# The beginning of a two-layer trunk: loads, squares and the order of the first norm

## Chip, cores, metric

One core of one Trainium2 chip. The metric is the device time of one execution in microseconds (us); the median of several runs is compared.

## What is computed

The reference runs two layers of a decoder trunk on x (1024 tokens by 1024 channels, float32). Each layer normalises x (`_rms`: x divided by the root of its mean square, times a gain per channel), projects it by one wide matrix, feeds three mixers (differential attention, a recurrent mixer, cross-attention to a memory of 256 tokens), gates and adds them, projects again and adds the result to x. Ahead of the cross-attention the memory is normalised and projected once for each layer:

```
h = _rms(x, norm_g[l]);  proj = h @ w_in[l]
mem_kv = _rms(mem, mem_norm_g[l]) @ w_mem_kv[l]
```

Only the beginning is touched by the change: the norm of x for the first layer and the memory's K and V for both layers.

## The kernel before, in words

The kernel is written with a scheduler that takes the operations in the order of the program, gives each a rank in that order, and lays out a fixed list for each engine from its own estimate of durations, the lowest rank first among what is ready. On the chip each engine works through its list in order and waits where an input is missing. `tc.high_priority()` sets the rank of what is inside back to that of the start of the program. Tensors are kept with the channels on the 128 partitions, x as 8 channel blocks (`NK`) of 1024 tokens, in two halves of 512 tokens.

Products are made in a split form: a float32 matrix becomes a rounded part `hi` (made by ACT, L178) and the rest `lo` (a subtraction, L171, on POOL or DVE), and `product` (L214) adds three matmuls for each channel block: hi by hi, hi by lo, lo by hi. `weight` (L204) loads 512 KB on the SP queue into `w_raw` and splits it into `w_hi` and `w_lo`; each of the three has two buffers, shared by all weights of the kernel, so the load of a third weight waits for the `w_lo` of the first, and the split of a third weight for the product of the first.

The prologue, ahead of both layers, does this in program order. (1) Eight loads of x on ACT's queue, each two channel blocks of half the tokens (512 KB). (2) `memory_load`: the small parameters `par`, the memory `mt` (1 MB) and the constants `con`, on SP's queue. (3) `gqk`, a product of two parameter columns on DVE, and `memory` for layer 0: `mh` on ACT and `ml` on DVE, eight times 128x256, the memory times its gain in split form. (4) The norm of x, a half at a time: ACT squares each channel block (L1143), PE sums the squares over the channels with matmuls by a column of ones (`token_sums`, four matmuls for each block, adding up over eight blocks in `ps_x`; the profile counts two records for each), DVE makes the reciprocal root of the mean (`rsqrt`, twelve small operations from `rs_v` to `h_r`), ACT and PE spread it over the partitions (`spread`, four transposes into `ps_rb`, a copy `rbs`), and `normed` makes for each block `h_t` on DVE, `hh` on ACT and `hl` on DVE, or on POOL for every third block. (5) `memory_norm`, the same for the memory, with squares added up on DVE (`acc`). (6) `memory` for layer 1. (7) `memory_kv` for each layer: eight weights, eight products of 24 matmuls with 256 columns, a copy out of PSUM (ACT, L401) and a multiplication by the norm (`kv`, DVE); `memory_store` normalises K, transposes V and stores both.

The weights and the PSUM copies of `memory_kv` already stand under `tc.high_priority()`. After the prologue comes layer 0, which begins with `project` of the first input weights: matmuls `ps_pj<-hh,w_hi` with 512 columns.

Of the kernel before, what the change touches and what calls it, by code (L numbers as in the profile page):

```python
# [11 lines left out]
F32 = mybir.dt.float32  # L12
# [3 lines left out]
AF = mybir.ActivationFunctionType  # L16
ALU = mybir.AluOpType
AX = mybir.AxisListType

P = 128  # L20
S = 1024
D = 1024
DEPTH = 2
NK = D // P
# [16 lines left out]
              caq=1, cak=1, daq=1, dak=1, sub=1)  # L41
PC, _o = {}, 0
# [88 lines left out]
def trunk(ctx, tc, io, out, layers=DEPTH, dump=None):  # L131
    nc = tc.nc
    PSUM, DRAM = bass.MemoryType.PSUM, bass.MemoryType.DRAM

    cp = ctx.enter_context(tc.tile_pool(name="cp", bufs=1))
# [6 lines left out]
    pa = ctx.enter_context(tc.tile_pool(name="pa", bufs=2, space=PSUM))  # L142
# [5 lines left out]
    par = cp.tile([P, DEPTH, NPAR], F32, name="par")  # L148
# [5 lines left out]
    ones = cp.tile([P, 1], F32, name="ones")  # L154
# [15 lines left out]
    def ttv(o, a, b, op, eng=None):  # L170
        (eng or nc.vector).tensor_tensor(o, a, b, op=op)  # L171

    def stt(o, a, s, b, op0, op1):
        nc.vector.scalar_tensor_tensor(o, a, s, b, op0=op0, op1=op1)  # L174

    def split(hi, lo, src, eng=None):

        nc.scalar.activation(hi, src, AF.Copy)  # L178
        ttv(lo, src, hi.bitcast(F32), ALU.subtract, eng)
# [20 lines left out]
    def weight(src, eng=None, wp=wp):  # L200
        raw = wp.tile([P, 8 * P], F32, name="w_raw", tag="w_raw", bufs=2)
        hi = wp.tile([P, 8 * P], F32R, name="w_hi", tag="w_hi", bufs=2)
        lo = wp.tile([P, 8 * P], F32R, name="w_lo", tag="w_lo", bufs=2)
        nc.sync.dma_start(raw, src.rearrange("p k c -> p (k c)"))  # L204
        split(hi, lo, raw, eng or nc.gpsimd)
        return (hi.rearrange("p (k c) -> p k c", k=src.shape[1]),
                lo.rearrange("p (k c) -> p k c", k=src.shape[1]))

    def product(ps, w, act, nk, cols, toks):

        n = 0
        for k in range(nk):
            for a, b in ((0, 0), (0, 1), (1, 0)):
                nc.tensor.matmul(ps, w[a][:, k, cols], act[b][:, k, toks],  # L214
                                 start=n == 0, stop=n == 3 * nk - 1)
                n += 1

    def half(h):
        return slice(h * 512, h * 512 + 512)
# [28 lines left out]
    def transpose(o, i):  # L248
        nc.tensor.transpose(o, i, ident)  # L249

    def token_sums(ps, sq, n, rhs, first=True, last=True):

        c = rhs.shape[-1]
        for j in range(n):
            nc.tensor.matmul(ps[:, j * c:(j + 1) * c], sq[:, j * P:(j + 1) * P], rhs,
                             start=first and j == 0, stop=last, skip_group_check=True)
# [16 lines left out]
    def spread(ps, col, n, c):  # L273

        b = tp.tile([P, 512], F32, name="spread", tag="ta", bufs=TA)
        bv = b[:, :n * P].rearrange("p (j c f) -> p j c f", j=n, c=c)
        nc.scalar.copy(bv, col.rearrange("p (j c) -> p j c", c=c).unsqueeze(3).to_broadcast([P, n, c, P // c]))
        for j in range(n):
            transpose(ps[:, j * P:(j + 1) * P], b[:, j * P:(j + 1) * P])

    def pcol(l, name, i=0):
        return par[:, l, PC[name][0] + i:PC[name][0] + i + 1]
# [13 lines left out]
    def normed(l, hf, x1, r, rp, hh, hl):  # L296

        rb = pg.tile([P, 512], F32, name="ps_rb", tag="g")
        spread(rb, r, 4, 1)
        rbs = rp.tile([P, 512], F32, name="rbs", tag="rbs")  # L300
        nc.scalar.copy(rbs, rb)
        yield
        for k in range(NK):
            t = tp.tile([P, 512], F32, name="h_t", tag="tb" if k % 2 else "ta", bufs=TB if k % 2 else TA)
            stt(t, x1[:, k, :], pcol(l, "g", k), rbs, ALU.mult, ALU.mult)
            split(hh[:, k, half(hf)], hl[:, k, half(hf)], t, nc.gpsimd if k % 3 == 2 else nc.vector)
            yield

    def mean_rsqrt(ss, n):

        r = tp.tile([P, 8], F32, name="h_r", tag="h_r")[:, :n]
        rsqrt(r, ss[:, :n], n, 1.0 / D, EPS)
        return r
# [42 lines left out]
    def memory_load(mp):  # L356

        mt = mp.tile([P, NK, M], F32, name="mt")
        nc.sync.dma_start(par, io["par"].rearrange("l p n -> p l n"))
        nc.sync.dma_start(mt, io["memT"])  # L360
        nc.sync.dma_start(con, io["con"])
        return mt
# [19 lines left out]
    def memory(mp, l, mt):  # L382

        mh = mp.tile([P, NK, M], F32R, name="mh", bufs=2)
        ml = mp.tile([P, NK, M], F32R, name="ml", bufs=2)
        for k in range(NK):
            g = pcol(l, "mg", k)
            nc.scalar.activation(mh[:, k, :], mt[:, k, :], AF.Copy, scale=g)
            stt(ml[:, k, :], mt[:, k, :], g, mh[:, k, :].bitcast(F32), ALU.mult, ALU.subtract)
        return mh, ml  # L390

    def memory_kv(mp, m, rbs, l):

        kv = mp.tile([P, 8, M], F32, name="kv", bufs=2)
        for j in range(8):
            with tc.high_priority():
                w = weight(io["w_mem"][l, j], nc.gpsimd)
            ps = pj.tile([P, 512], F32, name="ps_pj", tag="pj")[:, :M]
            product(ps, w, m, NK, slice(0, P), slice(0, M))
            with tc.high_priority():  # L400
                nc.scalar.copy(kv[:, j, :], ps)  # L401
            ttv(kv[:, j, :], kv[:, j, :], rbs, ALU.mult)
        return kv

    def memory_store(l, kv):

        ss = pg.tile([P, 512], F32, name="ps_ss", tag="g")
        for jj in range(2):
            sq = tp.tile([P, 512], F32, name="sq", tag="ta", bufs=TA)
            nc.scalar.activation(sq, kv[:, jj * 2:jj * 2 + 2, :].rearrange("p j m -> p (j m)"), AF.Square)  # L410
            token_sums(ss[:, jj * 4:], sq, 4, ones, first=jj == 0)
        r = tp.tile([P, 8], F32, name="m_r", tag="m_r")
        rsqrt(r, ss[:, :8], 8, 1.0 / P, EPS)
        for jj in range(2):
            rb = pg.tile([P, 512], F32, name="ps_rb", tag="g")
            spread(rb, r[:, jj * 4:jj * 4 + 4], 4, 1)
            js = slice(jj * 2, jj * 2 + 2)
            stt(kv[:, js, :].rearrange("p j m -> p (j m)"), kv[:, js, :].rearrange("p j m -> p (j m)"),
                gqk[:, l:l + 1], rb, ALU.mult, ALU.mult)
        for j in range(4, 8, 2):  # L420
            pt = pg.tile([P, 512], F32, name="ps_t", tag="g")
            for t in range(4):
                transpose(pt[:, t * P:(t + 1) * P], kv[:, j + t // 2, (t % 2) * P:(t % 2) * P + P])
            nc.vector.tensor_copy(kv[:, j:j + 2, :].rearrange("p j m -> p (j m)"), pt)
        for j in (0, 4):
            nc.gpsimd.dma_start(kv_d[l, j:j + 4].rearrange("j p m -> p j m"), kv[:, j:j + 4, :])
# [701 lines left out]
    h = new_h()  # L1128
    with tc.tile_pool(name="mem", bufs=1) as mm, tc.tile_pool(name="x0", bufs=2) as mp:
        x1s = [mp.tile([P, NK, 512], F32, name="x1") for _ in range(2)]  # L1130
        for hf in range(2):
            for k in range(0, NK, 2):
                nc.scalar.dma_start(x1s[hf][:, k:k + 2, :],
                                    io["xT"][k:k + 2].rearrange("k p s -> p k s")[:, :, half(hf)])
        mt = memory_load(mm)
        gqk = cp.tile([P, DEPTH], F32, name="gqk")
        ttv(gqk, par[:, :, PC["caq"][0]], par[:, :, PC["cak"][0]], ALU.mult)
        parts = [memory(mm, 0, mt)]
        for hf in range(2):
            ss = pa.tile([P, 512], F32, name="ps_x", tag="a")  # L1140
            for k in range(NK):
                sq = mp.tile([P, 512], F32, name="sq", bufs=3)
                nc.scalar.activation(sq, x1s[hf][:, k, :], AF.Square)  # L1143
                token_sums(ss, sq, 4, ones, first=k == 0, last=k == NK - 1)
            list(normed(0, hf, x1s[hf], mean_rsqrt(ss, 4), mp, *h))
        rbs = memory_norm(mm, mt)
        parts += [memory(mm, l, mt) for l in range(1, layers)]
        for l in range(layers):
            memory_store(l, memory_kv(mm, parts[l], rbs, l))

    for l in range(layers):
        q = prepare(l)
# [35 lines left out]
        if True:  # L1188
            with tc.tile_pool(name="kvp", bufs=1) as kp:
# [4 lines left out]
                with tc.tile_pool(name="cap", bufs=2) as mp:  # L1194
                    unit = cross_prepare(l, q, h, mp, 0)
                    run_later()
                    for i in range(4):
                        ahead = cross_prepare(l, q, h, mp, i + 1) if i < 3 else None
# [3 lines left out]
        with tc.tile_pool(name="dte", bufs=1) as te, tc.tile_pool(name="atp", bufs=2) as mp:  # L1202
# [17 lines left out]
            for i in range(4):  # L1220
                ahead = diff_prepare(l, q, h, mp, rope, i + 1) if i < 3 else None
# [3 lines left out]
        with tc.tile_pool(name="mgp", bufs=1) as mp1:  # L1225
# [8 lines left out]
            h = hn  # L1234
# [16 lines left out]
```

## Time and profile before

| what | value |
|---|---|
| median of 3 runs | 2776.12 us (2769.37 to 2777.94) |
| profiled execution, its own time | 2769.06 us |
| its span in the profile | 2767.3 us |
| mean granted clock of TensorE | 0.978 of full |
| PE busy | 2643.5 us, 96% |
| DVE, ACT, POOL busy | 1690.4, 986.6, 816.0 us |

The span is what the profile shows between the first and the last instruction. PE multiplies, PEld loads its weights, DVE is the vector engine, ACT the scalar engine, POOL the general engine, SP issues loads. A name with a q (ACTq, SPq) is the issuing sequencer. A share of busy time includes time in which an engine stands inside an instruction that has started.

### The profile page before, as it was taken

To read this page: it belongs to the slowest core of one execution; us is meant where nothing else is said; L and a number is where in the kernel's file an instruction comes from. 1 tells how busy PE (TensorE), PEld (TensorE's weight loads), DVE (VectorE), ACT (ScalarE), POOL (GpSimd) and SP (SyncE) were. 2 spreads that over 40 slices of the span, in tenths; PEclk is the share of its full clock that TensorE was granted. 3 is DMA by queue.
4 is the path that set the end of the run, shared out by engine and by line. 5 is a ranking of instruction groups with operands and counts; after the bars stand their busy time and mean duration, and the time that the engine had idled before them with its cause. 6 is when DMAs were issued, how large, how long until landed. Compare 5 with 4: busy or idle time off the path is not lost. (4 is left out here: it accounts for less than half of the span.)

```text
span 2767.3 us, 40395 instructions
## 1 busy us (share of the span) xinstructions
PE 2643.5 (96%) x15686; PEld 2144.8 (78%) x15686; DVE 1690.4 (61%) x3427; ACT 986.6 (36%) x1927; POOL 816.0 (29%) x716
## 2 busy tenths in 40 slices
PE   7799999999999999999999999999999999999999
PEld 7788788888876777777877778888887677777787
DVE  3748557557356777845556765656735577774552
ACT  4444322212232555722234432222223345573221
POOL 3445522232312222122234652123231222212210
PEclk8799999999999999999999999999999999999999
DMA  4323442322322112155352345223232211114534
GB/s 156 105 92 122 149 146 96 104 88 64 117 75 77 39 54 58 50 182 165 118 163 75 115 133 180 88 85 101 79 106 81 80 43 54 51 53 171 171 108 150
DMA packets 94479, 286.91 MB, mean 104 GB/s; under 512 B 12368, under 2 KB 19152, under 8 KB 91856
## 3 DMA queue, kind: packets, MB, share of 16 engines
q1 hardware_dynamic: 67088, 196.24, 23.5%
q0 software_dynamic: 25024, 83.90, 7.8%
q10 hardware_dynamic: 2176, 4.19, 0.4%
q8 instruction: 123, 2.02, 0.3%
q14 instruction: 68, 0.56, 0.1%
HBM read 198.31 MB, written 83.89 MB: 102 GB/s over the span
## 5 line engine op out<-in xcount | busy, mean ns | idle before, releaser
L171 POOL TENSOR_TENSOR w_lo<-w_raw,w_hi 128x1024 fp32r<-128x1024 f32 x170 | 421.2, 2478 | 937.5 <-ACT w_hi L178 891.1
L214 PE MATMUL ps_pj<-hh,w_hi 128*128 128x512 f32 x1568 | 634.5, 405 | 1.2 <-ACT hh L178 1.2
L214 PE MATMUL ps_pj<-hl,w_hi 128*128 128x512 f32 x1568 | 625.6, 399 | 1.2 <-DVE hl L171 1.2
L214 PE MATMUL ps_pj<-hh,w_lo 128*128 128x512 f32 x1568 | 622.9, 397 | 0.6 <-DVE w_lo L171 0.6
L178 ACT ACTIVATE w_hi<-w_raw 128x1024 fp32r<-128x1024 f32 x202 | 213.9, 1059 | 670.4 <-PE ps_pj L214 242.9
L214 PEld LDWEIGHTS ps_pj<-hl,w_hi 128*128 128x128 f32 x1568 | 298.1, 190 | 62.4 <-issue 4.3
L214 PEld LDWEIGHTS ps_pj<-hh,w_lo 128*128 128x128 f32 x1568 | 297.9, 190 | 61.7 <-issue 1.4
L214 PEld LDWEIGHTS ps_pj<-hh,w_hi 128*128 128x128 f32 x1568 | 297.7, 190 | 61.1 <-issue 2.9
L457 PE MATMUL ps_pj<-hh,w_hi 128*128 128x512 f32 x768 | 308.1, 401 | 0.0
L457 PE MATMUL ps_pj<-hl,w_hi 128*128 128x512 f32 x768 | 306.4, 399 | 0.0
L457 PE MATMUL ps_pj<-hh,w_lo 128*128 128x512 f32 x768 | 304.9, 397 | 0.0
L457 PEld LDWEIGHTS ps_pj<-hh,w_hi 128*128 128x128 f32 x768 | 146.5, 191 | 30.5
L457 PEld LDWEIGHTS ps_pj<-hh,w_lo 128*128 128x128 f32 x768 | 146.3, 190 | 30.4
L457 PEld LDWEIGHTS ps_pj<-hl,w_hi 128*128 128x128 f32 x768 | 146.5, 191 | 29.4
L1080 PE MATMUL ps_b<-yh,w_hi 128*128 128x512 f32 x384 | 147.5, 395 | 9.5 <-ACT yh L178 9.5
L1080 PE MATMUL ps_b<-yl,w_hi 128*128 128x512 f32 x384 | 152.7, 400 | 2.3 <-DVE misc L342 1.2
L1080 PE MATMUL ps_b<-yh,w_lo 128*128 128x512 f32 x384 | 150.5, 395 | 0.0
L981 ACT ACTIVATE de<-ps_d,dmx,des 128x512 f32<-128x512 f32 (+2 forms) x192 | 127.7, 670 | 50.7 <-DVE dmx L174 44.1
L171 DVE TENSOR_TENSOR rest<-sq 128x512 f32<-128x512 f32 x48 | 65.7, 1369 | 111.5 <-ACT sq L829 82.2
L974 DVE TENSOR_REDUCE dmx<-ps_d 128x1 f32<-128x512 f32 (+2 forms) x192 | 103.9, 551 | 23.1 <-PE ps_d L973 19.6
L442 POOL DMA_DIRECT2D g_d<-z_t x88 | 49.0, 557 | 213.3 <-ACT z_t L441 130.0
L171 DVE TENSOR_TENSOR inv_u<-inv_l,inv_x 128x126 f32<-128x126 f32 (+22 forms) x248 | 96.3, 388 | 16.4 <-ACT inv_l L670 9.6
(297 smaller groups left out, 4507.3 us busy)
## 6 DMA issues: line engine op xcount, KB each, us to landing
w_raw<-in_w_in_dram SPq DMA_DIRECT2D x130, 512.0 KB
g_d<-z_t POOLq DMA_DIRECT2D x88, 256.0 KB, 4.7
tg<-g_d SPq DMA_DIRECT2D x88, 256.0 KB
w_raw<-in_w_out_dram SPq DMA_DIRECT2D x32, 512.0 KB
z_d<-z_t POOLq DMA_DIRECT2D x48, 256.0 KB, 3.0
w_raw<-in_w_branch_dram SPq DMA_DIRECT2D x24, 512.0 KB
yr<-y_d SPq DMA_DIRECT2D x24, 512.0 KB
w_raw<-in_w_mem_dram SPq DMA_DIRECT2D x16, 512.0 KB
```

What stands on the lines that cost most here:

```text
L171: (eng or nc.vector).tensor_tensor(o, a, b, op=op)
L178: nc.scalar.activation(hi, src, AF.Copy)
L214: nc.tensor.matmul(ps, w[a][:, k, cols], act[b][:, k, toks], start=n == 0, stop=n == 3 * nk - 1)
L442: nc.gpsimd.dma_start(g_d[n, d][:, half(hf)], tg)
L457: nc.tensor.matmul(ps, w[a][:, k, :], h[b][:, k, half(hf)], start=n == 0, stop=n == 3 * NK - 1)
L974: nc.vector.tensor_reduce(mx[:, b:b + 1], ps[:, :n], axis=AX.X, op=ALU.max)
L981: nc.scalar.activation(e[:, b * 512:b * 512 + n], ps[:, :n], AF.Exp, scale=es[:, t, c:c + 1], bias=mx[:, 0:1], accum_out=ls[:, b:b + 1])
L1080: nc.tensor.matmul(pb, wb[a][:, i, (d % 2) * P:(d % 2) * P + P], b[i][:, half(hf)], start=k3 == 0, stop=k3 == 11)
```

## The change

All eight loads of x move from ACT's queue to SP's, behind the first two memory weights, the parameters, the memory and the constants. The first two memory weights are made ahead (`w0`) and handed to `memory_kv`. The squares of each half are added up on DVE into `acc` (the first square is written there), and PE sums once for each half instead of eight times. Loads, `gqk`, the first layer's `memory` and the whole norm of x stand under `tc.high_priority()`, and so have the ranks of the program's start.

```diff
-    def memory_kv(mp, m, rbs, l):
+    def memory_kv(mp, m, rbs, l, ahead=()):
...
             with tc.high_priority():
-                w = weight(io["w_mem"][l, j], nc.gpsimd)
+                w = ahead[j] if j < len(ahead) else weight(io["w_mem"][l, j], nc.gpsimd)
...
         x1s = [mp.tile([P, NK, 512], F32, name="x1") for _ in range(2)]
-        for hf in range(2):
-            for k in range(0, NK, 2):
-                nc.scalar.dma_start(x1s[hf][:, k:k + 2, :],
-                                    io["xT"][k:k + 2].rearrange("k p s -> p k s")[:, :, half(hf)])
-        mt = memory_load(mm)
-        gqk = cp.tile([P, DEPTH], F32, name="gqk")
-        ttv(gqk, par[:, :, PC["caq"][0]], par[:, :, PC["cak"][0]], ALU.mult)
-        parts = [memory(mm, 0, mt)]
-        for hf in range(2):
-            ss = pa.tile([P, 512], F32, name="ps_x", tag="a")
-            for k in range(NK):
-                sq = mp.tile([P, 512], F32, name="sq", bufs=3)
-                nc.scalar.activation(sq, x1s[hf][:, k, :], AF.Square)
-                token_sums(ss, sq, 4, ones, first=k == 0, last=k == NK - 1)
-            list(normed(0, hf, x1s[hf], mean_rsqrt(ss, 4), mp, *h))
+        with tc.high_priority():
+            w0 = [weight(io["w_mem"][0, j], nc.gpsimd) for j in range(2)]
+            mt = memory_load(mm)
+            for hf in range(2):
+                for k in range(0, NK, 2):
+                    nc.sync.dma_start(x1s[hf][:, k:k + 2, :],
+                                      io["xT"][k:k + 2].rearrange("k p s -> p k s")[:, :, half(hf)])
+            gqk = cp.tile([P, DEPTH], F32, name="gqk")
+            ttv(gqk, par[:, :, PC["caq"][0]], par[:, :, PC["cak"][0]], ALU.mult)
+            parts = [memory(mm, 0, mt)]
+            for hf in range(2):
+                acc = mp.tile([P, 512], F32, name="acc")
+                for k in range(NK):
+                    sq = mp.tile([P, 512], F32, name="sq", bufs=3)
+                    nc.scalar.activation(acc if k == 0 else sq, x1s[hf][:, k, :], AF.Square)
+                    if k:
+                        ttv(acc, acc, sq, ALU.add)
+                ss = pa.tile([P, 512], F32, name="ps_x", tag="a")
+                token_sums(ss, acc, 4, ones)
+                list(normed(0, hf, x1s[hf], mean_rsqrt(ss, 4), mp, *h))
         rbs = memory_norm(mm, mt)
...
-            memory_store(l, memory_kv(mm, parts[l], rbs, l))
+            memory_store(l, memory_kv(mm, parts[l], rbs, l, () if l else w0))
```

## Rows read from the trace of the kernel before

**Rows 1.** The head of the page.
```profile
span 2767.3 us, 40395 instructions
```

**Rows 2.** Windows: stretch and length, then busy us of each engine, clock, DMA share, GB/s.
```profile
9.90:49.10 39.20, 33.64 (x189) 33.62 (x189) 7.59 (x28) 15.45 (x30) 9.03 (x4) 0.87 0.43 155
49.10:127.30 78.20, 58.84 (x388) 56.63 (x387) 61.58 (x98) 39.22 (x71) 37.60 (x18) 0.78 0.29 93
...
140.00:200.00 60.00, 59.90 (x287) 48.92 (x287) 27.77 (x39) 27.61 (x47) 27.81 (x32) 1.00 0.25 80
```

**Rows 3.** PE's waits from 0 to 127.3: for whom, us, times, longest.
```profile
PE ps_pj L214 <- ACT mh L388: 15.5, 1, 15.5
PE ps_pj L214 <- DVE ml L174: 10.0, 1, 10.0
```

**Rows 4.** ACT in order of time: start, us, instruction, [idle before, releaser].
```profile
8.35 6.50 ACTq L1133 DMA_DIRECT2D x<-in_xT_dram  x5
...
26.27 1.06 ACT L178 ACTIVATE w_hi<-w_raw 128x1024 fp32r<-128x1024 f32 x1 [4.90 <-PE ps_pj L214]
...
44.87 0.61 ACT L277 COPY spread<-h_r 128x512 f32<-128x512 f32 x1
```

**Rows 5.** DVE in order of time.
```profile
9.97 1.86 DVE L171 TENSOR_TENSOR gqk<-par 128x2 f32<-128x2 f32 x1 [8.19 <-DMA par<-in_par_dram]
...
37.75 0.16 DVE L186 TENSOR_SCALAR rs_v<-ps_x 128x4 f32<-128x4 f32 x1 [19.03 <-PE ps_x L255]
...
39.93 0.16 DVE L174 SCALAR_TENSOR_TENSOR h_r<-rs_t,rs_i 128x4 f32<-128x4 f32 x1
49.16 2.74 DVE L174 SCALAR_TENSOR_TENSOR h_t<-x,par,rbs 128x512 f32<-128x512 f32 x4 [9.07 <-ACT rbs L301]
...
87.70 1.28 DVE L171 TENSOR_TENSOR hl<-h_t,hh 128x512 fp32r<-128x512 f32 x2
```

**Rows 6.** POOL in order of time.
```profile
9.47 2.34 POOL L171 TENSOR_TENSOR w_lo<-w_raw,w_hi 128x1024 fp32r<-128x1024 f32 x1 [0.86 <-ACT w_hi L178]
```

**Rows 7.** Groups of DVE and POOL from 49.1 to 127.3: busy, mean ns, idle before.
```profile
L174 DVE SCALAR_TENSOR_TENSOR h_t<-x,par,rbs 128x512 f32<-128x512 f32 x16 | 18.3, 1194 | 9.1 <-ACT rbs L301 9.1
L171 DVE TENSOR_TENSOR kv<-kv,m_rb 128x256 f32<-128x256 f32 x15 | 13.5, 955 | 4.6 <-ACT kv L401 2.9 <-ACT m_rb L379 1.6
L171 DVE TENSOR_TENSOR hl<-h_t,hh 128x512 fp32r<-128x512 f32 x12 | 10.7, 924 | 1.2 <-ACT hh L178 1.1
L174 DVE SCALAR_TENSOR_TENSOR ml<-mt,par,mh 128x256 fp32r<-128x256 f32 x8 | 4.7, 603 | 1.8 <-ACT mh L388 1.8
L171 DVE TENSOR_TENSOR acc<-acc,sq 128x256 f32<-128x256 f32 x7 | 2.9, 414 | 0.2
...
L171 POOL TENSOR_TENSOR w_lo<-w_raw,w_hi 128x1024 fp32r<-128x1024 f32 x12 | 29.6, 2465 | 29.4 <-ACT w_hi L178 29.3
L171 POOL TENSOR_TENSOR hl<-h_t,hh 128x512 fp32r<-128x512 f32 x4 | 6.5, 1630 | 8.0 <-ACT hh L178 8.0
```

**Rows 8.** PE in order of time.
```profile
16.57 0.41 PE L214 MATMUL ps_pj<-mh,w_hi 128*128 128x256 f32 x1
16.78 0.41 PE L214 MATMUL ps_pj<-ml,w_hi 128*128 128x256 f32 x1
...
36.02 1.70 PE L255 MATMUL ps_x<-ones,sq 128*128 128x1 f32 x8
...
47.55 0.95 PE L249 MATMUL ps_rb<-con,spread 128*128 128x128 f32 x4
...
127.26 0.47 PE L214 MATMUL ps_pj<-hh,w_hi 128*128 128x512 f32 x1
```

**Rows 9.** Windows, columns as in rows 2.
```profile
0.00:5.00 5.00, 0.00 (x0) 0.00 (x0) 0.74 (x9) 1.28 (x1) 0.21 (x4) 1.00 0.58 168
...
10.00:15.00 5.00, 0.00 (x0) 0.00 (x0) 2.33 (x8) 0.10 (x1) 1.81 (x1) 1.00 1.01 394
...
90.00:100.00 10.00, 7.87 (x33) 7.00 (x33) 7.79 (x19) 4.18 (x8) 4.73 (x2) 0.50 0.24 66
```

## The prediction

> **What bounds the kernel now.** I read the profile in five steps. First the span and the windows: the profiled execution spans 2767.3 us, and from 140 to 200 us TensorE (PE) is busy 59.90 of 60 us at full granted clock [rows 1, 2]. What comes later is a PE stretch that starts when the prologue releases it, so a microsecond by which the first input projection starts sooner is a microsecond off the end, if the order behind it stays. That first projection matmul (`ps_pj<-hh,w_hi`) starts at 127.26 us [rows 8]. The question is what sets 127.26.
>
> Second, PE's waits: 15.5 us until the first `mh` of the memory, and one wait of 10.0 us for `ml` of the second layer [rows 3]. PE itself is no bound here: between 49.1 and 127.3 us it is busy 58.84 of 78.20 us, partly at the lower clock [rows 2].
>
> Third, ACT in order of time: its sequencer is held from 8.35 us for 6.50 us by five loads of x, so nothing of its list runs; at 26.27 us it has waited 4.90 us for a memory product before a weight's `w_hi`, and the squares of x stand behind that in the same list [rows 4]. The reader should see that the squares, the sums on PE and the memory's weights hold one another up.
>
> Fourth, DVE: it stands idle 19.03 us before the first `rs_v` at 37.75, because the last sum of the first half of x comes so late; `h_t` begins only at 49.16 and the last `hl` ends at 88.98 [rows 5].
>
> Fifth, DVE against POOL. `gqk` multiplies two columns and takes 1.86 us, from 9.97 to 11.83; `w_lo` holds POOL from 9.47 to 11.81 [rows 5, 6]. So a DVE operation with two inputs stands still while POOL subtracts, and I treat the two as one resource, "the pair". Its work from 49.1 to 127.3 us, without the blocking: 16 `h_t` at 0.685 (four took 2.74) are 11.0; 12 `hl` at 0.64 are 7.7; 30 operations of 128x256 (`kv`, `ml`, `acc`) at 0.41 are 12.3; three reciprocal roots at 2.35 (37.75 to 40.09) are 7.0; POOL's 12 `w_lo` at 2.36 are 28.3 and its 4 `hl` at 1.6 are 6.4 [rows 5, 7]. That is 72.7 of 78.2 us, 93%. From 49 us on the pair sets the time, before that waiting does.
>
> **The change part by part.** *Loads on SP.* All are of known size: two weights of 0.52 MB, `par` about 0.06, `mt` 1.05, `con` 0.2, x 4.19. The kernel before moves 0.84 MB in its first 5 us and about 394 GB/s after [rows 9]. In one line, in the new order, 2.16 MB (to the end of `mt`) are there at 5 + 1.32/0.394 = 8.4 us, half of x (4.45 MB) at 14.2, all of x at 19.5; I add 0.6 us for the signal (an estimate; bounds 0 and 1). ACT no longer issues, so `mh` and PE start near 9 to 10 instead of 15.46: worth 5 to 6 us of PE, which is not the bound. The third weight's load now stands behind eight loads of x on SP and lands near 21 us; its `w_hi` then ends near 22.5, against a start at 26.27 before [rows 4], so this queueing costs nothing. Should one queue be slower than two, each 10% less rate puts x off by 1.5 us.
>
> *Sums.* Removed from PE: 16 groups of four small matmuls (eight records), 1.70 us each at the low clock [rows 8], about 20 us of PE time, of which two groups stay (records of the kernel before run at either clock, so less than 16 x 1.70). What matters is that squares no longer wait for PE. Added on DVE: 14 additions of 128x512 with two inputs in SBUF. The trace has none of that name; lower bound 0.64 (`hl`), upper 1.19 (the mean of `h_t` with its blocking) [rows 5, 7]; I take 0.68, 9.5 us, since POOL's third `w_lo` can't start before about 22 us and so can't block the first half's.
>
> *The chain ahead.* The first half's last pair of x lands at 14.8; two squares at 0.61 (ACT's 128x512 pass), an addition 0.68, the sums 1.70, the root 2.35, `spread` 0.61, four transposes 0.95, `rbs` 0.61 [rows 4, 5, 8]: 8.1 us together with nothing in front, so `h_t` starts at 23. Before, 11.4 us passed from `rs_v` to `h_t` against 4.5 of work [rows 5], so the upper bound is 30. I take 25. The second half's additions end by about 23 and mostly fit in front of it; I leave 1 us of them behind.
>
> *From there to the first projection*, two ways. By the pair: 72.7, plus three `w_lo` that before were done by 49 us and now are not (7.1), plus 1, is 80.8; at the same 93% it takes 86.9, so 112 us. By the sequence: `h_t` to the last `hl` took 39.8 us [rows 5]; the second half's sums, root and spread no longer stand inside it (about 7.5 less), two or so more `w_lo` do (5 more): 37, so 62 us; from the last `hl` to the first projection 38.3 us passed, with the second layer's eight products [rows 5, 8]: 100 us. Between ends of 100 and 112 I take 106, a gain of 21 us. The weights in advance for the first two products are no change of work: they already led SP's queue. The memory's K, V and stores now stand behind x on DVE and ACT; nobody before the first cross attention reads them, but the second layer's `ml` decides when eight products can run, and that is inside the 38.3.
>
> The Trainium skill's page "SBUF — State Buffer", section "Who interferes with whom", says that a DVE instruction with two SBUF inputs and a GpSimd instruction that reads SBUF exclude each other for a whole instruction, whichever began first. By that rule every one of the 14 additions loads the pair, and the pair sum above (112 us, gain 15) is the better of my two; the rows of `gqk` and `w_lo` agree with it.
>
> **The rivals.** *It packs better.* DVE and ACT have gaps while x lands; the second layer's `ml`, the memory's `acc` and root (3.3 + 2.9 + 2.35) could fill them, and `h_t` start at 23. The pair then has 72.3 us left and at 100% ends at 95: gain 32, 2744 us; up to ten more if the first layer's `kv` passes also fall behind the projection. For it: the memory's data is there at 9. Against it: in the kernel before `ml` had the same freedom and was still late.
>
> *PE's clock.* Without the sums PE pauses between products, and the granted clock may stay at the lower level (1.2 of 2.4 GHz), as in 90 to 100 us, 0.50, after a pause [rows 3, 9]. A product of 24 matmuls then takes 24 x 0.21 = 5.1 us [rows 8]; 16 of them 82, some 10 of sums and transposes, and 18 us of waits, from 9.7: 120 us, gain 7, 2769. It decides from the point where PE's own time passes the pair's. The Trainium skill's page "TensorE: Matmul & The Clock Gate", section "HAM oscillation", says that waits between bursts of matmuls bring the low clock back; it would speak for this case.
>
> *The change does not do what it says.* The memory's weights carry the same mark, with the earliest rank, so `w_hi` may still stand in front of the squares on ACT, waiting for a product, as at 26.27 [rows 4]. One such weight puts `h_t` off by about 8 us, two or three use up the gain: 2772 to 2778.
>
> *Slower.* The pair, over the whole stretch from 9.9 to 127.3 us, was busy 7.6 + 9.0 + 72.7 = 89.3 of 117.4 us, 76% [rows 2, 7]. If lists of fixed order keep waiting for each other at that share, 89.3 + 9.5 = 98.8 takes 130 us from 9.9: the projection at 140, 13 us later, 2789. It decides below a share of 79%. Against it: the idle share was waiting for the sums.
>
> **How the numbers follow.** The profiled execution took 2769.06 us, 7 less than the median of 2776.12; a gain of 21 makes 2748 and 2755. 0.3% (8.3 us) is about what a measurement of this kernel can tell from no change. Chances: the forecast (2749 to 2762) 0.50; better packing (2735 to 2748) 0.17; the clock (2762 to 2772) 0.13; not done 0.10; slower 0.10. Faster by over 0.3%: 0.50 + 0.17 + half of the clock, 0.73; slower 0.10; the same 0.17. The range 2736 to 2773 leaves out the slower case, half of "not done" and a tail of the best: 0.8 inside.
>
> **What would show it.** Right: x wholly landed by 20 us, the first PE matmul before 11, `h_t` from 23 to 30, the last `hl` in 58 to 72, the first `hh` matmul in 100 to 112 and the same PE density behind it. Wrong: squares on ACT behind a `w_hi` that waits; 0.50 as the clock of most of 20 to 100; gaps on both DVE and POOL at once; or a first projection at 106 and an unmoved end, which would mean that the later order changed.

## The result, and the profile after

The median is 2744.48 us (2736.57 to 2751.1, four runs) against 2774.78 us of the kernel before (2769.37 to 2777.94, four runs): a ratio of 0.9892, 95% interval 0.9861 to 0.9922. That is 30 us, or 1.1%. The forecast was 2755. One execution of the study, of e3's kernel below, took 5122.95 us and is left out of its ratio. The profiled execution took 2744.38 us, and this is the head of its page:

```profile
span 2742.6 us, 40195 instructions
```

The span is 24.7 us shorter than in [rows 1]. The windows of [rows 2], for the changed kernel:

```profile
9.90:49.10 39.20, 28.84 (x183) 27.48 (x183) 32.34 (x50) 24.62 (x48) 17.24 (x8) 0.91 0.57 193
49.10:127.30 78.20, 61.64 (x362) 54.70 (x363) 63.10 (x107) 32.56 (x57) 36.53 (x19) 0.88 0.32 103
140.00:200.00 60.00, 59.90 (x283) 47.93 (x282) 40.85 (x54) 32.80 (x57) 30.16 (x32) 1.00 0.28 92
```

The third busy time in each line is DVE's. It has 32.34 us in the first stretch where it had 7.59, part of which is standing beside POOL; PE has less there and more in the second stretch, because the first projections now lie in it; the granted clock is 0.91 and 0.88 instead of 0.87 and 0.78. From 140 us PE is as dense as before, 59.90 of 60.

SP's own queue in order of time shows how the loads were really placed:

```profile
0.76 0.86 SPq L204 DMA_DIRECT2D w_raw<-in_w_mem_dram  x2
...
3.12 0.45 SPq L1136 DMA_DIRECT2D x<-in_xT_dram  x1
8.01 2.63 SPq L204 DMA_DIRECT2D w_raw<-in_w_mem_dram  x2
10.69 1.45 SPq L1136 DMA_DIRECT2D x<-in_xT_dram  x3
20.12 0.34 SPq L204 DMA_DIRECT2D w_raw<-in_w_mem_dram  x1
20.50 0.43 SPq L1136 DMA_DIRECT2D x<-in_xT_dram  x1
...
37.93 0.43 SPq L1136 DMA_DIRECT2D x<-in_xT_dram  x1
```

The loads do not go out in one line. The memory's further weights, which have the rank of the program's start as well, stand between them, and each of those waits for a buffer, that is, for a `w_lo` on POOL. SP's waits from 0 to 60 us (for whom, us, times, longest):

```profile
SPq L204 <- POOL w_lo L171: 41.1, 9, 7.6
```

Seven of eight loads of x stand behind such a weight; the last is issued at 37.93 us, while ACT had issued all of them by 14.85 [rows 4]. So the move makes x *later*, and the time still falls.

DVE in order of time, against [rows 5]:

```profile
20.69 8.86 DVE L171 TENSOR_TENSOR acc<-acc,sq 128x512 f32<-128x512 f32 x6
...
33.62 0.49 DVE L174 SCALAR_TENSOR_TENSOR ml<-mt,par,mh 128x256 fp32r<-128x256 f32 x1 [0.54 <-ACT mh L388]
...
35.20 2.33 DVE L174 SCALAR_TENSOR_TENSOR h_r<-rs_t,rs_i 128x4 f32<-128x4 f32 x1
...
39.63 4.18 DVE L174 SCALAR_TENSOR_TENSOR h_t<-x,par,rbs 128x512 f32<-128x512 f32 x3
...
87.25 3.47 DVE L171 TENSOR_TENSOR hl<-h_t,hh 128x512 fp32r<-128x512 f32 x2
```

`h_t` starts at 39.63 instead of 49.16, and the last `hl` ends at 90.7: no sooner than the 88.98 of before. Six additions take 8.86 us, 1.48 each. The last `ml` of the second layer ends at 34.1 us. In the kernel before it came after x's `h_t`:

```profile
90.71 0.47 DVE L174 SCALAR_TENSOR_TENSOR ml<-mt,par,mh 128x256 fp32r<-128x256 f32 x1
```

What came sooner is PE. Its waits up to 127.3 us, against [rows 3]:

```profile
PE ps_pj L214 <- POOL w_lo L171: 13.9, 11, 2.6
PE ps_pj L214 <- ACT mh L388: 11.0, 1, 11.0
PE ps_rb L249 <- ACT spread L277: 5.8, 3, 2.8
PE ps_x L255 <- DVE acc L171: 4.7, 2, 3.8
```

The start comes 4.5 us sooner, the wait for the second layer's `ml` is gone, and the wait for `w_lo` has grown (2.4 us before). Now PE's groups up to the first projection matmul. First the kernel before, 0 to 127.3 us (busy, mean ns, idle before):

```profile
L214 PE MATMUL ps_pj<-ml,w_hi 128*128 128x256 f32 x128 | 44.1, 346 | 10.0 <-DVE ml L174 10.0
...
L255 PE MATMUL ps_x<-ones,sq 128*128 128x1 f32 x128 | 20.7, 283 | 2.6 <-ACT sq L1143 2.6
L249 PE MATMUL ps_rb<-con,spread 128*128 128x128 f32 x18 | 4.0, 355 | 4.2 <-ACT spread L277 4.2
L255 PE MATMUL ps_ss<-ones,sq 128*128 128x1 f32 x32 | 3.7, 242 | 0.0
L249 PE MATMUL ps_t<-con,kv 128*128 128x128 f32 x8 | 1.9, 421 | 0.0
```

Then the changed kernel, 0 to 95.2 us:

```profile
L214 PE MATMUL ps_pj<-mh,w_lo 128*128 128x256 f32 x128 | 42.1, 329 | 13.1 <-POOL w_lo L171 13.1
...
L255 PE MATMUL ps_x<-ones,acc 128*128 128x1 f32 x16 | 2.7, 292 | 4.7 <-DVE acc L171 4.7
L249 PE MATMUL ps_rb<-con,spread 128*128 128x128 f32 x8 | 1.3, 287 | 0.3 <-ACT spread L277 0.3
```

The first `hh` matmul starts at 95.19 us (127.26 before), 32.1 us sooner. In both kernels PE stands idle for nothing just ahead of it, so it is PE's own list, its work and its waits, that sets its start. The groups account for it: 4.5 from the earlier start; 10.0 from `ml`; the sums, 20.7 + 2.6 before and 2.7 + 4.7 now, 15.9; spreads, and the memory's sums and transposes, of which the memory's part before came ahead of that matmul and now mostly does not, 4.0 + 4.2 + 3.7 + 1.9 against 1.3 + 0.3, 12.2; less 11.7 for the waits on the weights' split (14.3 now, 2.6 before). That is 30.9 of 32.1; PE's busy time for the products themselves is about 1 us shorter, at the higher clock.

Not all of it lasts. The first pass on ACT behind the input projections (`lw`, L489) comes at 142.9 us (162.9 before), 20.0 sooner, and the first store of `y_d` at 500.1 (518.0), 17.9 sooner. The 12 us between are what moved and was not saved: the memory's tail (its norm, K's norm, V's transposes) now stands in the middle of the projections. PE in order of time there:

```profile
95.19 0.40 PE L214 MATMUL ps_pj<-hh,w_hi 128*128 128x512 f32 x1
...
101.08 0.44 PE L249 MATMUL ps_rb<-con,spread 128*128 128x128 f32 x2 [2.82 <-ACT spread L277]
101.28 0.57 PE L214 MATMUL ps_pj<-hh,w_lo 128*128 128x512 f32 x1
...
105.01 0.95 PE L255 MATMUL ps_ss<-ones,sq 128*128 128x1 f32 x8
```

From the first store of `y_d` to the end, the profiles of all fourteen kernels of this study took from 2240.6 to 2254.1 us. So of the 24.7 us of the span about 18 are the beginning, and the rest is within what single executions scatter later. I use that first store as the mark of what a beginning is worth. It is read from one execution of each kernel, and not always a typical one: the profiled execution of before lay 5.7 us under its median, that of e8 14.7 and that of e11 6.3 us above theirs.

### The profile page after: what moved, and what is told of

Read it like the earlier page. It is cut to its first block, busy times and chain, and to the rows that moved or that the text cites. A ratio compares the mean times of both kernels' runs of the same rounds, so it can differ in the third digit from the quotient of the medians.

```text
span 2742.6 us, 40195 instructions
## 1 busy us (share of the span) xinstructions
PE 2620.3 (96%) x15574; PEld 2119.9 (77%) x15574; DVE 1711.4 (62%) x3441; ACT 985.2 (36%) x1927; POOL 817.3 (30%) x716
## 5 line engine op out<-in xcount | busy, mean ns | idle before, releaser
L457 PEld LDWEIGHTS ps_pj<-hh,w_hi 128*128 128x128 f32 x768 | 147.2, 192 | 30.9
L457 PEld LDWEIGHTS ps_pj<-hl,w_hi 128*128 128x128 f32 x768 | 147.0, 191 | 29.7
L171 DVE TENSOR_TENSOR inv_u<-inv_l,inv_x 128x126 f32<-128x126 f32 (+22 forms) x248 | 96.2, 388 | 16.4 <-ACT inv_l L670 9.6
```

The lines of the kernel that those rows point to most:

```text
L457: nc.tensor.matmul(ps, w[a][:, k, :], h[b][:, k, half(hf)], start=n == 0, stop=n == 3 * NK - 1)
```

## The experiments

Theories put into the expectations: **A**, the sums on PE block the memory's products, and taking them away is the gain. **B**, the loads and the chain of the norm come ahead, and that is the gain. **C**, POOL's subtractions stop DVE, and the pair of them sets the prologue. **D**, the memory's tail, pushed behind the first projections, takes part of the gain back. Ratios are to the kernel before, which was measured again beside each set of runs (medians 2771.8 for e1 to e4, 2777.85 for e5 to e8, 2773.06 for e9 to e12), so ratios compare better across sets than medians do. The columns from the first `hh` on are start times in us.

| run | median us | ratio (95%) | first `hh` | `lw` | first `y_d` store |
|---|---|---|---|---|---|
| before | 2774.78 | 1 | 127.3 | 162.9 | 518.0 |
| after | 2744.48 | 0.9892 (0.9861 to 0.9922) | 95.2 | 142.9 | 500.1 |
| e1 | 2750.45 | 0.9918 (0.9891 to 0.9945) | 107.8 | 146.0 | 501.9 |
| e2 | 2752.03 | 0.9924 (0.9896 to 0.9951) | 96.7 | 140.9 | 497.9 |
| e3 | 2764.71 | 0.9977 (0.9959 to 0.9996) | 117.5 | 161.8 | 518.7 |
| e4 | 2750.24 | 0.9921 (0.9894 to 0.9949) | 106.2 | 150.0 | 507.7 |
| e5 | 2727.53 | 0.9835 (0.981 to 0.9861) | 67.5 | 127.9 | 483.7 |
| e6 | 2747.12 | 0.99 (0.9868 to 0.9932) | 104.9 | 143.2 | 501.4 |
| e7 | 2742.89 | 0.9884 (0.986 to 0.9908) | 96.3 | 137.7 | 495.7 |
| e8 | 2720.68 | 0.9813 (0.9784 to 0.9841) | 98.3 | 128.0 | 486.1 |
| e9 | 2751.84 | 0.9913 (0.9882 to 0.9943) | 99.1 | 143.3 | 500.3 |
| e10 | 2732.89 | 0.985 (0.9822 to 0.9879) | 81.9 | 126.3 | 484.1 |
| e11 | 2742.62 | 0.988 (0.985 to 0.9911) | 90.4 | 140.6 | 494.2 |
| e12 | 2724.06 | 0.9824 (0.9795 to 0.9852) | 66.7 | 122.1 | 479.1 |

**e1: the kernel before with the sums alone.**

```diff
-            ss = pa.tile([P, 512], F32, name="ps_x", tag="a")
+            acc = mp.tile([P, 512], F32, name="acc")
...
-                token_sums(ss, sq, 4, ones, first=k == 0, last=k == NK - 1)
+                if k:
+                    ttv(acc, acc, sq, ALU.add)
+            ss = pa.tile([P, 512], F32, name="ps_x", tag="a")
+            token_sums(ss, acc, 4, ones)
```

> The kernel before, with one part of the change: the squares of x are added on DVE, PE sums once a half. Loads, ranks and queues are those of before. Theory A (PE's list: the sums of x stood between the memory's products and made squares, weights and products wait for one another): 10 to 20 us faster than before, about 2755 to 2765, with the first hh matmul near 110. Theory B (the gain comes from the loads and from the norm's rank ahead of the memory's work): within 8 us of before, about 2775, first hh matmul near 127.

It gave 0.9918, some 22.7 us, more than A's 10 to 20, and the first store 16.1 us sooner, while its loads and ranks are those of before. B alone is out; the sums are enough for most of the gain.

**e2: the changed kernel with the sums on PE again** (the reverse of that edit).

> The changed kernel, but with the sums of x on PE as before (eight groups of four matmuls for each half). Theory A: most of the gain is lost, 2760 to 2775. Theory B: the gain stays, 2740 to 2750, and the first hh matmul is near 95 to 100.

A expected most of the gain to be lost. It kept 0.9924, and the first store is 20.1 us sooner than before. So either half of the change gives nearly the whole by the first store, and over two thirds of it by the ratios: the sums are no necessary cause. This half holds the loads, the early rank and the weights made ahead together; the loads alone, in the code of before, were not run. The window from 10 to 50 us shows PE close to full, 39.22 of 40 us, with the sums in it:

```profile
10.00:50.00 40.00, 39.22 (x310) 37.99 (x310) 26.11 (x42) 26.58 (x51) 17.62 (x9) 1.00 0.58 197
```

**e3: the kernel before with `memory` of both layers ahead of the norm of x.**

```diff
-        parts = [memory(mm, 0, mt)]
+        parts = [memory(mm, l, mt) for l in range(layers)]
...
-        parts += [memory(mm, l, mt) for l in range(1, layers)]
```

> The kernel before, with one line moved: the memory times its gain is made for both layers ahead of the norm of x, so that ml of the second layer does not stand behind the norm on DVE. Theory A in its second part (the 10.0 us wait of PE for that ml was part of what was gained): 6 to 12 us faster than before, 2763 to 2769. Theory B: within 8 us, about 2775.

The wait of 10.0 us for `ml` is gone from PE's list, and the first `hh` matmul comes 9.8 us sooner. Yet the median falls by 6 to 7 us only (0.9977), at the low end of A's band and still within B's 8, `lw` comes 1.1 us sooner, and the first store does not come sooner at all: an earlier first projection is worth little by itself. My reading is that the memory's sums, spread and transposes then follow it and cost what was won.

**e4: the changed kernel with the loads of x on POOL's queue.**

```diff
-                    nc.sync.dma_start(x1s[hf][:, k:k + 2, :],
+                    nc.gpsimd.dma_start(x1s[hf][:, k:k + 2, :],
```

> The changed kernel, with the eight loads of x issued on POOL's queue, where no weight's load stands among them. All of x should land by about 22 us and h_t start near 27 instead of 39.6. Theory B: another 8 to 12 us faster than the changed kernel, 2733 to 2737. Theory A: within 6 us of the changed kernel, 2739 to 2750, as the first projection waits for the memory's sixteen products, not for the norm.

Four loads of x are issued from 1.29 us. `h_t` starts at 32.7 instead of 39.6 and the last `hl` starts at 81.9 instead of 90.0, as B wanted. But `mt` lands later, the first matmul waits until 15.2 us (11.0), the first `hh` comes 11.0 us *later* and the first store 7.6 us later. This is the clearest miss for B: the chain of the norm came 7 to 8 us sooner and the beginning took longer. It does not test the norm alone, since PE's start moved with it by 4.2 us; and by the medians the run can't be told from the changed kernel (0.9921 against 0.9892, intervals overlap).

**e5: the changed kernel with the memory weights' `w_lo` on DVE.**

```diff
-                w = ahead[j] if j < len(ahead) else weight(io["w_mem"][l, j], nc.gpsimd)
+                w = ahead[j] if j < len(ahead) else weight(io["w_mem"][l, j], nc.vector)
...
-            w0 = [weight(io["w_mem"][0, j], nc.gpsimd) for j in range(2)]
+            w0 = [weight(io["w_mem"][0, j], nc.vector) for j in range(2)]
```

> The changed kernel, with the memory weights' w_lo subtracted on DVE instead of POOL. Theory C (DVE and POOL exclude each other, and their joint time sets the prologue): sixteen subtractions of 2.36 us of POOL become about 1.23 us of DVE each (the same shape elsewhere on DVE), 18 us less for the pair, and the first lora pass on ACT (142.9 in the changed kernel) comes 8 to 15 us sooner, 2728 to 2737 us. Theory D (the memory's products follow one another by waiting times, or the memory's norm and store at the end hold PE): within 6 us of the changed kernel.

C's number came, at the good end of its band: 2727.53 us, `lw` 15.0 us and the first store 16.4 us sooner than in the changed kernel. DVE's groups from 0 to 145 us, first of the changed kernel, then of e5:

```profile
L171 DVE TENSOR_TENSOR acc<-acc,sq 128x512 f32<-128x512 f32 x14 | 17.8, 1270 | 2.3 <-ACT sq L1145 1.4
L171 DVE TENSOR_TENSOR hl<-h_t,hh 128x512 fp32r<-128x512 f32 x12 | 16.6, 1407 | 0.0
```

```profile
L171 DVE TENSOR_TENSOR w_lo<-w_raw,w_hi 128x1024 fp32r<-128x1024 f32 x16 | 19.4, 1220 | 2.4 <-ACT w_hi L178 2.3
...
L171 DVE TENSOR_TENSOR acc<-acc,sq 128x512 f32<-128x512 f32 x14 | 9.7, 689 | 1.4 <-ACT sq L1145 0.9
L171 DVE TENSOR_TENSOR hl<-h_t,hh 128x512 fp32r<-128x512 f32 x12 | 8.9, 772 | 0.0
```

The 14 additions cost 9.7 instead of 17.8 us and the 12 `hl` 8.9 instead of 16.6. A `w_lo` itself takes 1.22 us on DVE against 2.53 on POOL, and PE's wait for it falls from 13.9 us to 3.7. The run moves both at once: DVE is no longer stopped, and the split is quicker. Which of the two gives how much is not separated.

**e6: the changed kernel with the memory's norm ahead of the norm of x.**

```diff
             parts = [memory(mm, 0, mt)]
+            rbs = memory_norm(mm, mt)
...
-        rbs = memory_norm(mm, mt)
```

> The changed kernel, with the memory's own norm (squares, root, spread) traced ahead of the squares of x, so that K's and V's multiplications, norm and store do not gather behind the norm of x. Theory D (in the changed kernel 12 of the 32 us by which the first hh matmul comes sooner are lost again by 143 us, since PE's list holds the memory's spreads, sums and transposes between the first projections): the lora pass 4 to 10 us sooner than 142.9, 2734 to 2740 us. Theory C: no change or worse by the norm of x starting later, 2742 to 2752.

No gain: 0.99, and `lw` at 143.2, so D's forecast failed and C's band holds. The tail is not saved by being done earlier; the first `hh` is later by 9.7 us, and `lw` comes when it came.

**e7: the changed kernel without the mark around loads, `memory` and norm.**

```diff
-        with tc.high_priority():
+        if True:
```

> The changed kernel without the outer high_priority: loads on SP's queue and sums on DVE stay, the rank is the program's. If the rank moves the norm of x ahead, this loses 5 us or more against the changed kernel (2750 and above) and h_t starts after 42. If the program's order had put it ahead already, the same as the changed kernel within 6 us, and h_t near 39.6.

0.9884 against 0.9892: no difference, and `h_t` starts at 39.0. The order of the program already put these operations early; the rank part of the change does nothing that shows. The first store is 4.4 us sooner here and `lw` 5.2, so a difference of that size between two single profiles should not be read as an effect.

**e8: the changed kernel without the memory's tail.** It leaves out the memory's norm and its multiplication, K's norm and V's transposes, and stores the raw products.

```diff
-            ttv(kv[:, j, :], kv[:, j, :], rbs, ALU.mult)
...
+        for j in (0, 4):
+            nc.gpsimd.dma_start(kv_d[l, j:j + 4].rearrange("j p m -> p j m"), kv[:, j:j + 4, :])
+        return
...
-        rbs = memory_norm(mm, mt)
+        rbs = None
```

> The changed kernel without the memory's norm: K and V are stored as the sixteen products give them, without the multiplication by the memory's norm, the norm of K and the transposes of V. Theory D: this is all that holds PE between the first hh matmul and the lora pass, which then follows it by about 28 us (five and a half products of 24 matmuls by 0.228 us) instead of 47.7; 2722 to 2732 us. Theory C: DVE loses some 20 us of work, but what sets the first hh matmul (POOL's w_lo and the norm of x) stays; the lora pass is 4 to 8 us sooner, 2735 to 2741.

From the first `hh` to `lw` 29.7 us pass instead of 47.7, all of it PE work (131 matmuls at 0.227 us; the expectation's five and a half products at 0.228 make 30, not 28). `lw` comes 14.9 us and the first store 14.0 us sooner than in the changed kernel, in the slowest of its five executions (2735.36 us). D holds here: the tail costs about 15 us. That it costs as much wherever it stands is what e3 and e6 suggest, where the first `hh` moved by 10 us and `lw` by 1 or less.

**e9: the kernel before with nothing but `w_lo` on DVE** (the first line of e5's edit, in the code of before).

> The kernel before, with nothing but the memory weights' w_lo moved from POOL to DVE. Theory C (POOL's w_lo stops DVE's two-input instructions, whatever they are): the twelve w_lo of 2.47 us that run beside h_t, hl and kv from 49 to 127 us become instructions of 1.1 to 1.2 us on DVE, so the first lora pass on ACT comes 12 to 18 us sooner than 162.9, at 145 to 151, and the time is 2755 to 2762 us. Rival (it paid 16 us in the changed kernel only because DVE carries the 14 additions there; in the kernel before the squares' sums on PE still set the beginning): the lora pass at 157 or later and 2768 to 2776 us.

0.9913 and the first store 17.7 us sooner, more than C asked in `lw` (19.6 us) and in time. By the first store, this one word in the kernel before is worth as much as the whole change (17.7 and 17.9 us); by the ratios it is somewhat less, with overlapping intervals. DVE's groups from 0 to 145 us:

```profile
L171 DVE TENSOR_TENSOR w_lo<-w_raw,w_hi 128x1024 fp32r<-128x1024 f32 x16 | 19.4, 1218 | 17.5 <-ACT w_hi L178 17.5
L174 DVE SCALAR_TENSOR_TENSOR h_t<-x,par,rbs 128x512 f32<-128x512 f32 x16 | 13.4, 870 | 2.9 <-ACT rbs L301 2.9
```

The 16 `h_t` take 13.4 us where they took 18.3 [rows 7].

**e10: e1 and e9 together**, without the move of the loads.

> The kernel before with the squares summed on DVE and the memory weights' w_lo on DVE; the loads of x stay on ACT's queue and nothing is moved ahead. Theory: once DVE is not stopped by POOL, the loads on SP still free ACT's sequencer and the second layer's ml, 3 to 8 us: 2731 to 2738 us, behind the 2727.5 us of the changed kernel with w_lo on DVE. Rival (the loads' move was worth something only through that blocking): 2724 to 2730 us, no different from it.

2732.89 us lies in the band of the first theory, but the trace speaks for the rival: the first store is at 484.1 us and in e5 at 483.7, and the intervals (0.9822 to 0.9879, 0.981 to 0.9861) overlap. With sums and `w_lo` on DVE, moving the loads adds nothing that can be measured.

**e11: e2 and e9 together**, the loads moved and `w_lo` on DVE, the sums on PE.

> The changed kernel with the sums of squares on PE again (per block, as in the kernel before) and the memory weights' w_lo on DVE. Theory: PE was busy 39.2 of 40 us from 10 to 50 us in the run with PE sums, so PE is what that stretch waits for, and w_lo on DVE gains less than the 16 us that it gained with the sums on DVE: 4 to 12 us on 2752.0, 2740 to 2748. Rival (the pair of DVE and POOL sets the stretch here as well): 12 to 18 us, 2734 to 2740.

9.4 us by the medians, 12 by the ratios, 3.7 by the first store: the first theory's band by the medians, and its upper end by the ratios. From 10 to 50 us PE is busy all the time, at a lower granted clock, 0.73:

```profile
10.00:50.00 40.00, 39.93 (x240) 39.71 (x240) 14.08 (x33) 20.32 (x39) 0.00 (x0) 0.73 0.56 190
...
25.00:30.00 5.00, 5.00 (x25) 5.00 (x25) 0.00 (x0) 1.09 (x3) 0.00 (x0) 0.50 0.35 111
```

The clock is a rival that this run does not rule out. In e2 it was 1.00 over the same 40 us, with 310 matmuls done against 240 here; here it fell to 0.50 from 25 to 35 us although PE never paused, and the profiled execution was the slowest of six. How much of the small gain at the first store is the full PE and how much the clock of this one execution stays open.

**e12: e5 with x's `hl` of the prologue all on DVE.**

```diff
-            split(hh[:, k, half(hf)], hl[:, k, half(hf)], t, nc.gpsimd if k % 3 == 2 else nc.vector)
+            split(hh[:, k, half(hf)], hl[:, k, half(hf)], t, nc.gpsimd if l and k % 3 == 2 else nc.vector)
```

> The changed kernel with the memory weights' w_lo on DVE, and x's hl of the prologue all on DVE too, so that POOL subtracts nothing there. Theory C: four hl of 1.63 us on POOL, 6.5 us in which DVE's two-input instructions stand, become four of 0.64 to 0.77 us on DVE: 2 to 4 us sooner than 2727.5, 2723 to 2726. Rival (DVE is now full in its own right, and four more subtractions lengthen it): 2728 to 2732.

2724.06 us, 0.9824; the first store is 4.6 us sooner than in e5, though the two medians cannot be told apart. It is the best complete version of the study, some 20 us under the changed kernel. It also shows C most plainly: up to 65 us POOL does nothing but four constants, and `hl` takes 0.64 to 0.69. Then the next weights' `w_lo` begin, on POOL still:

```profile
65.40 2.58 POOL L171 TENSOR_TENSOR w_lo<-w_raw,w_hi 128x1024 fp32r<-128x1024 f32 x1 [64.94 <-ACT w_hi L178]
```

```profile
49.74 2.07 DVE L174 SCALAR_TENSOR_TENSOR h_t<-x,par,rbs 128x512 f32<-128x512 f32 x3
...
63.64 4.88 DVE L174 SCALAR_TENSOR_TENSOR h_t<-x,par,rbs 128x512 f32<-128x512 f32 x4 [0.62 <-ACT rbs L301]
```

Three `h_t` at 49.74 take 2.07 us; four at 63.64, across that `w_lo`, take 4.88, 2.1 more than four at 0.69.

## Why the prediction was right, and where not

The sign was right, and the size roughly: 21 us forecast, 30 by the medians, about 18 by the part of the profile that the change touches. The way there was largely another, and that the total came near is partly luck: a gain at the first projection that was put too small (21 against 32.1) met a loss behind it that the sum did not have (12). Of the signs named for "right", only the dense PE behind the projection came; the first matmul, at 11.00, just missed. The time lies below the forecast's own band, in that of the rival "it packs better" (2735 to 2748). That rival said that the second layer's `ml` would fill DVE's gaps while x lands, that `kv` passes would fall behind the projection, and that this would start at 95; all three came. Its `h_t` at 23 did not, so its 95 too was reached by another way.

**Loads.** "In one line, all of x at 19.5" failed. The last load is issued at 37.93, because further weights stand between the loads and wait for their buffers. The text had the third weight queue behind eight loads of x; the queue did the opposite. The rival "does not do what it says" named the weights' same early rank, but looked for it in ACT's list, where up to 60 us no `w_hi` waits for a product; it showed in SP's queue. Its price was wrong, because it took `h_t` for what counts. The 0.6 us for the signal is an estimate that no row measures, and small beside this. ACT's early start was right: `mh` at 10.44 against 9 to 10, the first matmul at 11.00.

**`h_t` at 25, the last `hl` at 62.** They came at 39.63 and 90.7. Of the 16.7 us between 22.9, the chain with nothing in front, and 39.63, 12.9 lie ahead of the end of the first half's additions (29.55 against 16.7): later loads, squares that ACT does in turn with `mh` and `w_hi`, and additions at twice their price. The other 3.9 lie in the root, which took 6.2 us with `ml` between its steps and a blocked `h_r`.

**The additions** at 0.68 each, 9.5 us: they took 1.27, 17.8 us, above my upper bound of 1.19. The step that failed is "POOL's third `w_lo` can't start before about 22 us": it started at 17.70, and the next two fall into the six additions from 20.69 to 29.55. POOL in order of time:

```profile
17.70 2.39 POOL L171 TENSOR_TENSOR w_lo<-w_raw,w_hi 128x1024 fp32r<-128x1024 f32 x1 [7.42 <-ACT w_hi L178]
21.02 2.60 POOL L171 TENSOR_TENSOR w_lo<-w_raw,w_hi 128x1024 fp32r<-128x1024 f32 x1 [0.93 <-ACT w_hi L178]
26.66 2.34 POOL L171 TENSOR_TENSOR w_lo<-w_raw,w_hi 128x1024 fp32r<-128x1024 f32 x1 [3.04 <-ACT w_hi L178]
35.13 2.39 POOL L171 TENSOR_TENSOR w_lo<-w_raw,w_hi 128x1024 fp32r<-128x1024 f32 x1 [6.13 <-ACT w_hi L178]
```

With `w_lo` off POOL they take 0.689 (e5), so the unblocked price was right and the blocking was left out.

**The first projection at 106, by either of two ways.** It came at 95.19. Both ways took the norm of x for what releases it, and "PE itself is no bound here" put PE's relief at nothing. That failed: PE comes to that matmul without a pause, the sums taken off PE are 15.9 of the 32.1 us, and the matmul reads the first half of x alone, whose `hl` were done by 57.8 us. The 38.3 us behind the last `hl` were a distance in time and not a wait; they are 4.5 us now. With the second layer's `ml` done by 34.1 us instead of 91.2, the 16 products no longer wait for the norm of x. In e4 an earlier norm brought no earlier projection. The gain was then given back in part, which the sum did not have: PE behind the first projection was not "unchanged", since the memory's tail moved there, 12 us. e8, which leaves that tail out, has `lw` 14.9 us sooner.

**The pair of DVE and POOL.** The one resource by which I counted is borne out by e5, e9 and e12, with the reserve stated under what stays open: taking POOL's `w_lo` away gains 16 us in the changed kernel, by the first store and by the ratios, and in the kernel before 18 by the first store and 24 by the ratio. What I did not see is that the two halves of the change would not add up. By the first store: sums 16.1 us (e1), loads 20.1 (e2), both 17.9. With `w_lo` on DVE: that alone 17.7 (e9), with the sums 33.9 (e10), close to 16.1 + 17.7, with the loads 23.8 (e11), with both 34.3 (e5). My reading is that sums on PE fill PE up to 50 us (e2, e11) and sums on DVE fill the pair, so that only moving `w_lo` frees the second; the loads' part is covered by one or the other. This is argued from single profiles and not shown: of its numbers the 23.8 is open to e11's clock.

**The clock** was no cost. The rival expected half speed over most of the stretch; the granted clock rose in both windows, from 0.87 to 0.91 and from 0.78 to 0.88.

**Rank.** The early rank of loads and norm does nothing that shows (e7), so that part of the change was not needed.

The Trainium skill's page "SBUF — State Buffer", section "Who interferes with whom", which the prediction weighed, has the later instruction blocked until the other is done. The rows agree, the length too: `h_r`, four columns, takes 2.33 us at 35.20 beside the `w_lo` of 2.39 at 35.13 shown above, and 0.16 without one [rows 5].

Open: how much of e5's gain is the quicker `w_lo` and how much the freed DVE. Open too are the 12 us between the 30 of the medians and the 18 of the first store: some 6 of them lie in that the profiled execution of before was under its median (2769.06 against 2774.78), the later stretch scatters by 13 us between the profiles, and no run here says whether a part of it is the change's. A hint that it may be: that stretch averages 2250.4 us over the five profiles with the sums on PE and 2243.6 over the nine with the sums on DVE, though the two groups overlap. Open last is e11's clock.

## What to carry to other kernels

Find what the bound engine does and waits for, not the longest chain: here the norm's chain ended no sooner and the time still fell, and in e4 it ended sooner and nothing was won. Before spreading elementwise work over DVE and POOL, price the pair as one: if POOL takes twice as long and stops DVE meanwhile, moving the subtraction to the "busier" DVE can be a gain, here, by the first store, as large as a reordering of the whole beginning. And of two edits that relieve the same stretch, run each alone; the second may be free of effect.

## What the runs showed of the hardware that was not expected

POOL's subtraction stops DVE instructions with a single tensor input as well. In the changed kernel, on DVE and POOL in order of time:

```profile
7.92 0.16 DVE L331 TENSOR_SCALAR misc<-par 128x13 f32<-128x13 f32 x1
8.00 2.31 DVE L333 TENSOR_SCALAR misc<-par 128x4 f32<-128x4 f32 x1
...
94.44 0.16 DVE L186 TENSOR_SCALAR rs_v<-ps_ss 128x2 f32<-128x2 f32 x1 [0.70 <-PE ps_ss L255]
94.64 1.93 DVE L187 TENSOR_SCALAR rs_i<-rs_v 128x2 int32<-128x2 int32 x1
...
97.00 2.23 DVE L174 SCALAR_TENSOR_TENSOR rs_t<-rs_t,rs_v 128x2 f32<-128x2 f32 x1
```

```profile
5.64 4.64 POOL L171 TENSOR_TENSOR w_lo<-w_raw,w_hi 128x1024 fp32r<-128x1024 f32 x2 [5.18 <-ACT w_hi L178]
...
94.16 2.37 POOL L171 TENSOR_TENSOR w_lo<-w_raw,w_hi 128x1024 fp32r<-128x1024 f32 x1 [4.59 <-ACT w_hi L178]
96.80 2.41 POOL L171 TENSOR_TENSOR w_lo<-w_raw,w_hi 128x1024 fp32r<-128x1024 f32 x1 [0.26 <-ACT w_hi L178]
```

Four columns take 2.31 us, two columns 1.93, each until POOL is done; 0.16 is what such an operation takes alone. The one at 7.92 starts as the first of the two `w_lo` ends, which may be why it got through. The one at 94.44 reads PSUM, and takes 0.16 inside a `w_lo`. The one at 97.00 has two tensors as inputs. The operation at 94.64 is a shift by a constant, so its one tensor is all that it reads. The Trainium skill says in the same section of "SBUF — State Buffer" that `tensor_scalar` can enter modes that take the ports shared with GpSimd, when its operands meet certain conditions; these rows agree, while the prediction had counted instructions with two inputs alone. The pair at 94.64 and 97.00 adds 3.8 us to the memory's root, and the 2.82 us for which PE stands before `ps_rb` at 101.08 lie at the end of that chain. A few columns at the wrong moment cost over three times what a free 128x512 operation does (0.69).
